# Binding the four decay differences of the SSD branch to fixed places in VectorE's queue

## The chip, the cores and the metric

The kernel runs on one core of one Trainium2 chip. The metric is the device time of one execution in microseconds, the median of several executions.

The core has five engines with a queue each: TensorE (PE in the profile; its weight loads are listed as PEld) does matrix products and transposes from SBUF into PSUM, VectorE (DVE) and ScalarE (ACT) do elementwise work, GpSimd (POOL) a few small operations, SyncE (SP) issues most DMAs.

## The reference

The network has two layers. Each is a half-step SwiGLU feed-forward part (FFN), a mixer and a second FFN; at the end stands an RMS norm. There are 256 tokens of width 1024, all in float32. The mixer runs a Mamba-2 branch (SSD) and a gated DeltaNet branch on the same input and adds their gated outputs. What matters here is the SSD branch, with 32 heads in 4 groups of 8, and two chunks of 128 tokens:

```python
a_cum = jnp.cumsum(log_a, axis=2)
seg = a_cum[:, :, :, None] - a_cum[:, :, None, :]
decay = jnp.where(causal, jnp.exp(jnp.where(causal, seg, 0.0)), 0.0)
cb = jnp.einsum("bclgn,bcsgn->bclsg", Cc, Bc)
y_diag = jnp.einsum("bclsg,bclsgh,bcsghp->bclghp", cb, decay, xdt)
...
return (y_diag + y_off).reshape(b, S, H, P)
```

For each head and chunk, `seg` is the difference of every two cumulated log decays; its exponential, masked to the causal half, is multiplied with the product of C and B, and that matrix is applied to the tokens.

## The kernel before, in words

**Weights.** All weights come from DRAM as a stream of 128 x 1024 tiles (`wraw`, 512 KB each, five buffers). Each tile is split into a rounded high part (`whi`, ScalarE, L68) and the remainder (`wlo`, VectorE, L71), so that three reduced-precision matmuls stand for one float32 matmul. High and low parts have five buffers each (`NSPL`). A tile is loaded and split ahead of its use by `take` (L202): when tile j is taken, tile j+4 is prepared. A new split thus waits until TensorE is through with the tile five before it.

**The order of the work.** A mixer is a list of small steps, `ORDER` (L46), that `step` (L1209) runs one by one. Its end, which matters here, reads `P g100 g101 D0 S0 x10 T0 D1 x11 g110 g111 S1 x20 T1 o x21 N D2 y S2 D3 x30 x31 T2 g000 g010 g001 S3 g011 T3`:

- `P` (`ssd_pre`, L1038) makes the four products of C and B (`cbb` in PSUM, L1045 and L1046). For each group VectorE masks two blocks into `cbm` (tile `cbt`, L1047), ScalarE copies a third (L1053).
- `D` and a group number (`decay`, L1059) makes that group's decay: a DMA spreads 1 MB of cumulated logs over all partitions (L1061), then come four steps over 128 x 2048 elements: the difference (VectorE, L1065), the minimum with 0 (VectorE, L1071), the exponential (ScalarE, L1072) and the product with `cbm` (VectorE, L1073). All are done in place in the tile `dc`. Groups 0 and 2 share one slot, groups 1 and 3 another.
- `S` and `T` (`ssd`, L1087) are the head and the rest of a group: transposes of the convolved input (`xsb`, L1101), three scalings (`xD`, `xdt`, `xe`), then 64 small matmuls per group that read `dc` (`ydb`, L1115), sums and a norm.
- `x` (`xs_unit`, L1076) projects half a group's input (tensor `xs`) and convolves it: for each 128 channels ScalarE starts `ca`, VectorE adds three taps (L634), ScalarE applies SiLU into `xsT` (L635). `g` (`gate`, L1141) projects a piece of a gate (PSUM name `t`).
- `o` and `N` (`dn_T`, L1150, and `dn_branch`, L1197) bring the DeltaNet result through its output matrix: four pieces are transposed (`oT`), normalised and gated (`og`) and split into `bh` (ScalarE) and `bl` (VectorE, L1160), and each pair feeds 24 matmuls into `b` (L335 to L337). The sums are gated into `tg` (L1203).
- `y` (`ss_T(0)`, L1163) transposes the first piece of the SSD result (`yT`, L1169) for its own output matrix.

The DeltaNet recurrence (`recur`, L945) ends around `P`: `ob` (L995) is added to its other part in `vb` (L998), and that addition frees a PSUM bank. The transposes and small products share four such banks (`trp`).

**What sets the order within an engine.** The code is traced once, in the order of the steps, and a scheduler then writes a fixed queue for each engine at build time. By its own estimate of times it lets the earliest traced instruction go first among those whose inputs are ready, so a later step can stand ahead of an earlier one that is not ready. `tc.issue_after(ins)` is a context: instructions of `ins`'s engine that are traced inside it stand behind `ins` in that engine's queue. It orders the queue alone and adds no semaphore. On the chip each queue is worked off in its order.

Of the kernel before, what the change touches and what calls it, by code (L numbers as in the profile page):

```python
# [11 lines left out]
ALU = mybir.AluOpType  # L12
# [4 lines left out]
P = 128  # L17
D = 1024
S = 256
# [34 lines left out]
def trunk_kernel(ctx, tc, x, wst, wsm, norms, lpar, rpar, cst, out):  # L54
    nc = tc.nc
    V, A, G, PE = nc.vector, nc.scalar, nc.gpsimd, nc.tensor
# [10 lines left out]
    def act(o, i, func=AF.Copy, **kw):  # L67
        return A.activation(out=o, in_=i, func=func, **kw)  # L68

    def tt(o, a, b, op):  # L70
        return V.tensor_tensor(out=o, in0=a, in1=b, op=op)  # L71

    def stt(o, a, s, b, op0, op1):
        return V.scalar_tensor_tensor(out=o, in0=a, scalar=s, in1=b, op0=op0, op1=op1)

    def ts(o, a, s1, op0, sc2=None, op1=None):
        if op1 is None:
            return V.tensor_scalar(out=o, in0=a, scalar1=s1, scalar2=None, op0=op0)
# [70 lines left out]
    state = {"loaded": 0, "prepped": 0, "taken": 0, "last": None, "hold": False, "behind": {}, "late": {}, "first": 0, "turns": {}, "first_chunk": False, "cap": n_forms}  # L149
# [69 lines left out]
    h = cpool.tile([P, 2, D], F32, name="h")  # L219
# [11 lines left out]
    ident = cs[:, 0:P]  # L231
# [361 lines left out]
    def mixer(l, nxt):  # L593
# [13 lines left out]
        yz = {}  # L607
# [37 lines left out]
        ac = small([P, 2, 40], "ac", 1)  # L645
# [380 lines left out]
        late = {}  # L1026
# [11 lines left out]
        def ssd_pre():  # L1038
            BT, CT = late["BC"][:, 0:4], late["BC"][:, 4:8]
            cbt = slots.tile([P, 3 * GS, P], F32, tag="sF", name="cbt")  # L1040
            late["cbx"] = cbx = cbt[:, 2 * GS :]
            late["cbm"] = cbm = cbt[:, : 2 * GS].rearrange("p (g t) l -> p g t l", g=GS)
            for g in range(GS):
                cbb = trb("cbb")
                PE.matmul(cbb[:, 0 : 2 * P], BT[:, g, 0:P], CT[:, g, :], start=True, stop=True)  # L1045
                PE.matmul(cbb[:, 2 * P : 3 * P], BT[:, g, P : 2 * P], CT[:, g, P : 2 * P], start=True, stop=True)  # L1046
                tt(  # L1047
                    cbm[:, g],
                    cbb[:].rearrange("p (t o l) -> p t o l", t=2, o=2)[:, :, 0, :],
                    U[:, None, :].to_broadcast([P, 2, P]),  # L1050
                    ALU.mult,
                )
                act(cbx[:, g], cbb[:, P : 2 * P])  # L1053
            yield

        xsT = {}
# [2 lines left out]
        def decay(g):  # L1059
            dc = slots.tile([P, 8, 2, P], F32, tag=("sA", "sB")[g % 2], name="dc")  # L1060
            nc.sync.dma_start(  # L1061
                dc[:].rearrange("p h t l -> p (h t l)"),
                rdram[8 * g : 8 * g + 8].rearrange("a b -> (a b)").partition_broadcast(P),
            )
            tt(  # L1065
                dc[:], dc[:],
                ac[:, :, 8 * g : 8 * g + 8].rearrange("p t h -> p h t")[:, :, :, None].to_broadcast([P, 8, 2, P]),
                ALU.subtract,
            )
            dv = dc[:].rearrange("p h t l -> p (h t l)")  # L1070
            ts(dv, dv, 0.0, ALU.min)  # L1071
            act(dv, dv, AF.Exp)  # L1072
            tt(dc[:], dc[:], late["cbm"][:, g, None].to_broadcast([P, 8, 2, P]), ALU.mult)  # L1073
            decs[g] = dc

        def xs_unit(g, i):  # L1076
# [73 lines left out]
        def dn_T(hp):  # L1150
            bank = trb("oT")
            bv = bank[:].rearrange("p (a c i) -> p a c i", a=2, c=4)
            for c in range(4):
                PE.transpose(bv[:, :, c, :], vb[:, c, hp, :], ident)
            og = tmp2("og")
            stt(og[:], bank[:], dnw, late["zdT"][:, 2 * hp : 2 * hp + 2, :].rearrange("p h t -> p (h t)"), ALU.mult, ALU.mult)
            oh = s2.tile([P, 2, S], F32R, tag="s2", name="bh")
            ol = s2.tile([P, 2, S], F32R, tag="s2", name="bl")
            act(oh[:].rearrange("p a t -> p (a t)"), og[:])
            tt(ol[:].rearrange("p a t -> p (a t)"), og[:], f(oh[:]).rearrange("p a t -> p (a t)"), ALU.subtract)  # L1160
            brT[("d", hp)] = (oh, ol)

        def ss_T(j):  # L1163
            bank = trb("yT")
            g, k0 = j // 2, (j % 2) * 2
            for k in range(2):
                for t in range(2):
                    c0 = (k0 + k) * P
                    PE.transpose(bank[:, k * S + t * P : k * S + (t + 1) * P], yz[g][:, t, c0 : c0 + P], ident)  # L1169
            oh = s2.tile([P, 2, S], F32R, tag="s2", name="bh")  # L1170
            ol = s2.tile([P, 2, S], F32R, tag="s2", name="bl")
            for k in range(2):
                w = snw[:, 2 * j + k : 2 * j + k + 1]
                act(oh[:, k], bank[:, k * S : (k + 1) * S], scale=w)
                stt(ol[:, k], bank[:, k * S : (k + 1) * S], w, f(oh[:, k]), ALU.mult, ALU.subtract)
            brT[("s", j)] = (oh, ol)

        def branch(kind, n, mk, tail=1):
            ps = [[accb("b"), accb("b")] for _ in range(2)]
            held = {}  # L1180

            def stat(k, t):
                oh, ol = held[k // 2]
                return oh[:, k % 2, t * P : (t + 1) * P], ol[:, k % 2, t * P : (t + 1) * P]

            made = 1
            for j0 in list(range(n - tail)) + [n - tail]:
                js = range(j0, j0 + (tail if j0 == n - tail else 1))
                while made < min(js[-1] + 2, n):
                    mk(made)  # L1190
                    made += 1
                for j in js:
                    held[j] = brT.pop((kind, j))
                out_chunks(ps, stat, [2 * j + i for j in js for i in range(2)], 2 * n - 1, group=2 * len(js))
            return ps

        def dn_branch():  # L1197
            ps = branch("d", 4, dn_T)
            m = tg[1]
            for t in range(2):  # L1200
                for n in range(2):
                    sl = slice(n * 512, (n + 1) * 512)
                    stt(m[:, t, sl], m[:, t, sl], 1.0, ps[t][n][:], ALU.add, ALU.mult)  # L1203
# [235 lines left out]
```

## Time and profile before

| | |
|---|---|
| median of 3 runs | 1543.27 us (1543.04 to 1545.02) |
| the profiled execution | 1541.48 us |
| its span, first to last instruction | 1539.7 us |
| granted TensorE clock | 0.999 |
| busy TensorE | 1522.8 us (99%) |
| busy VectorE | 1229.7 us (80%) |
| busy ScalarE | 944.8 us (61%) |

Times in the trace count from the start of the span. The end of the mixer in question lies at about 380 to 540 us in layer 0 and at 1141 to 1301 us in layer 1, with the same queues. A row in time gives the start, the duration, the engine, the line, the operation, what is written from what, and in brackets the idle time ahead of it with what ended that. A row of the chain that ended last has start, duration, engine, name and line. Small helpers record most operations, so that L71 stands for every `tt`, L68 for every `act`, L74 for every `stt` and L78 for `ts`: the names of the tiles tell them apart. For `dc`, `dc<-dc,ac` is the difference, `dc<-dc` on VectorE the minimum, `dc<-dc` on ScalarE the exponential and `dc<-dc,cbt` the product.

### The profile page before, as it was taken

The numbers are of one execution on the slowest core, as the hardware profiler recorded it, in microseconds if no ns is written. First come the engines' busy times: TensorE is split into PE (matmuls) and PEld (weight loads), VectorE is DVE, ScalarE is ACT, GpSimd is POOL, SyncE is SP. The second block draws the span as 40 slices with busy tenths as digits, with TensorE's granted clock in tenths as the row PEclk, the third lists the DMA queues.
The fourth block names the chain that finished last, engine by engine and source line by source line (L and its number), as shares of the span: only waits on it lengthen the run. The fifth ranks groups of instructions, "written<-read, shape, count | busy, mean of one in ns | idle before, by whom it ended". The sixth has DMA issues, their size and how long they took to land.

```text
span 1539.7 us, 29072 instructions
## 1 busy us (share of the span) xinstructions
PE 1522.8 (99%) x11473; PEld 1384.4 (90%) x11473; DVE 1229.7 (80%) x1859; ACT 944.8 (61%) x1532; POOL 81.8 (5%) x92
## 2 busy tenths in 40 slices
PE   8999999999999999999999999999999999999998
PEld 7999889999888888999899998899998888899997
DVE  6878769967899766789778887689589996677886
ACT  5655667765665645555555566676756666455565
POOL 0000110000000000000100012010000000000010
PEclk9999999999999999999999999999999999999999
DMA  7687775653565556587867687665345555556785
GB/s 277 190 265 231 226 228 167 187 164 111 178 213 171 163 166 196 185 256 211 261 225 225 208 253 229 197 193 180 117 141 202 179 170 186 176 177 195 247 241 156
DMA packets 98831, 305.73 MB, mean 199 GB/s; under 512 B 22837, under 2 KB 23813, under 8 KB 97670
## 3 DMA queue, kind: packets, MB, share of 16 engines
q1 hardware_dynamic: 93796, 290.95, 57.2%
q0 software_dynamic: 4608, 12.58, 5.1%
q8 instruction: 90, 1.47, 0.4%
q14 instruction: 47, 0.39, 0.1%
q10 hardware_dynamic: 290, 0.33, 0.1%
HBM read 297.72 MB, written 1.92 MB: 195 GB/s over the span
## 4 chain that ended last, share of the span: by engine, by line
PE 89%; DVE 4%; ACT 2%; DMA 2%; issue 1%; SPq 1%; POOL 0%; POOLq 0%; ACTq 0%; DVEq 0%
PE fc L346 10%; PE fc L340 9%; PE fc L345 9%; PE t L366 9%; PE o L337 4%; PE o L335 4%; PE o L336 4%; PE f L366 3%; PE b L335 3%; PE b L337 3%; PE b L336 3%; PE p L336 2%; PE p L337 2%; PE p L335 2%; PE xs L345 1%; PE xs L340 1%
## 5 line engine op out<-in xcount | busy, mean ns | idle before, releaser
L71 DVE TENSOR_TENSOR wlo<-wraw,whi 128x1024 fp32r<-128x1024 f32 x488 | 591.8, 1221 | 186.7 <-ACT whi L68 172.2
L68 ACT ACTIVATE whi<-wraw 128x1024 fp32r<-128x1024 f32 x488 | 511.6, 1059 | 271.0 <-PE fc L345 92.5
L346 PE MATMUL fc<-uW,wlo 128*128 128x256 f32 x1280 | 354.9, 277 | 0.0
L340 PE MATMUL fc<-uW,whi 128*128 128x256 f32 x1280 | 354.1, 277 | 0.0
L345 PE MATMUL fc<-uW,whi 128*128 128x256 f32 x1260 | 348.3, 276 | 0.0
L340 PEld LDWEIGHTS fc<-uW,whi 128*128 128x128 f32 x1280 | 240.5, 188 | 0.8
L346 PEld LDWEIGHTS fc<-uW,wlo 128*128 128x128 f32 x1280 | 240.5, 188 | 0.0
L345 PEld LDWEIGHTS fc<-uW,whi 128*128 128x128 f32 x1260 | 236.5, 188 | 0.8
L366 PE MATMUL t<-whi,uW 128*128 128x512 f32 x512 | 165.3, 397 | 0.0
L366 PEld LDWEIGHTS t<-whi,uW 128*128 128x128 f32 x512 | 95.9, 188 | 21.6 <-issue 1.3
L68 ACT ACTIVATE whi<-wsum 128x1024 fp32r<-128x1024 f32 x64 | 68.0, 1062 | 58.8 <-PE fc L345 32.9
L366 PE MATMUL t<-wlo,uW 128*128 128x512 f32 x256 | 100.2, 392 | 0.0
L71 DVE TENSOR_TENSOR wlo<-wsum,whi 128x1024 fp32r<-128x1024 f32 x64 | 78.2, 1221 | 7.9 <-ACT whi L68 5.6
L335 PE MATMUL b<-whi,bh 128*128 128x512 f32 x192 | 76.1, 398 | 0.3
L336 PE MATMUL b<-wlo,bh 128*128 128x512 f32 x192 | 74.9, 390 | 0.0
L337 PE MATMUL b<-whi,bl 128*128 128x512 f32 x192 | 74.2, 393 | 0.0
L340 PE MATMUL xs<-uW,whi 128*128 128x256 f32 x256 | 72.8, 284 | 0.0
L346 PE MATMUL xs<-uW,wlo 128*128 128x256 f32 x256 | 71.4, 279 | 0.0
L345 PE MATMUL xs<-uW,whi 128*128 128x256 f32 x254 | 70.6, 278 | 0.0
L335 PE MATMUL o<-whi,gh 128*128 128x512 f32 (+1 forms) x160 | 62.0, 388 | 0.0
L337 PE MATMUL o<-whi,gl 128*128 128x512 f32 (+1 forms) x160 | 61.8, 386 | 0.0
L336 PE MATMUL o<-wlo,gh 128*128 128x512 f32 (+1 forms) x160 | 61.7, 386 | 0.0
(337 smaller groups left out, 3291.7 us busy)
## 6 DMA issues: line engine op xcount, KB each, us to landing
wraw<-in_wst_dram SPq DMA_DIRECT2D x504, 512.0 KB, 4.9
wsum<-in_wst_dram SPq DMA_DIRECT2D x16, 512.0 KB, 7.3
wsum<-in_wst_dram POOLq DMA_DIRECT2D x16, 512.0 KB, 8.7
dc<-rdram SPq DMA_DIRECT2D x8, 1024.0 KB, 8.5
nw<-in_norms_dram SPq DMA_DIRECT2D x6, 512.0 KB, 5.9
h<-u POOLq DMA_DIRECT2D x12, 256.0 KB, 6.8
gb<-rdram SPq DMA_DIRECT2D x8, 256.0 KB, 5.6
h<-in_x_dram SPq DMA_DIRECT2D x4, 256.0 KB, 3.7
```

Source lines behind the costliest of these rows:

```text
L68: return A.activation(out=o, in_=i, func=func, **kw)
L71: return V.tensor_tensor(out=o, in0=a, in1=b, op=op)
L335: PE.matmul(ps, lh, rh, start=start, stop=False)
L336: PE.matmul(ps, lh, rl, start=False, stop=False)
L337: return PE.matmul(ps, ll, rh, start=False, stop=stop)
L340: PE.matmul(ps, wh, mh, start=start, stop=False)
L345: PE.matmul(ps, wh, ml, start=False, stop=False)
L346: PE.matmul(ps, wl, mh, start=False, stop=stop)
L366: ins = PE.matmul(ps[t][:], st, mv, start=k0 == 0 and j == 0, stop=k0 == KT - 2 and j == 5)
```

## The change

Two names carry instructions between the steps: `late["branch"]` and `late["diff"]`. The difference of group 0 is bound behind the fourth masked product of C and B, that of group 1 behind the minimum of group 0, that of group 2 behind the fourth `bl` of the DeltaNet branch, and that of group 3 behind the last product of group 2. The four transposes of `ss_T(0)` are bound behind the last matmul of the DeltaNet branch's sums. The computation is unchanged.

```diff
@@ ssd_pre
-                tt(
+                ins = tt(
                     cbm[:, g],
...
                 act(cbx[:, g], cbb[:, P : 2 * P])
+                if g == 3:
+                    late["branch"] = ins
@@ decay
-            tt(
-                dc[:], dc[:],
...
-                ALU.subtract,
-            )
+            with ExitStack() as behind:
+                behind.enter_context(tc.issue_after((late["diff"] if g == 1 else late["branch"]).ins))
+                tt(
+                    dc[:], dc[:],
...
+                    ALU.subtract,
+                )
             dv = dc[:].rearrange("p h t l -> p (h t l)")
-            ts(dv, dv, 0.0, ALU.min)
+            late["diff"] = ts(dv, dv, 0.0, ALU.min)
             act(dv, dv, AF.Exp)
-            tt(dc[:], dc[:], late["cbm"][:, g, None].to_broadcast([P, 8, 2, P]), ALU.mult)
+            late["branch"] = tt(dc[:], dc[:], late["cbm"][:, g, None].to_broadcast([P, 8, 2, P]), ALU.mult)
@@ dn_T
-            tt(ol[:].rearrange("p a t -> p (a t)"), og[:], f(oh[:]).rearrange("p a t -> p (a t)"), ALU.subtract)
+            ins = tt(ol[:].rearrange("p a t -> p (a t)"), og[:], f(oh[:]).rearrange("p a t -> p (a t)"), ALU.subtract)
             brT[("d", hp)] = (oh, ol)
+            if hp == 3:
+                late["branch"] = ins
@@ ss_T
-                    PE.transpose(bank[:, k * S + t * P : k * S + (t + 1) * P], yz[g][:, t, c0 : c0 + P], ident)
+                    with ExitStack() as behind:
+                        if j == 0:
+                            behind.enter_context(tc.issue_after(late["sums"].ins))
+                        PE.transpose(bank[:, k * S + t * P : k * S + (t + 1) * P], yz[g][:, t, c0 : c0 + P], ident)
@@ dn_branch
             ps = branch("d", 4, dn_T)
+            late["sums"] = state["sums"][-1]
```

More of the change, by code (lines that the diff above doesn't have):

```diff
@@ L1064, in decay @@
             )
-            tt(
-                dc[:], dc[:],
-                ac[:, :, 8 * g : 8 * g + 8].rearrange("p t h -> p h t")[:, :, :, None].to_broadcast([P, 8, 2, P]),
-                ALU.subtract,
-            )
+            with ExitStack() as behind:
+                behind.enter_context(tc.issue_after((late["diff"] if g == 1 else late["branch"]).ins))
+                tt(
+                    dc[:], dc[:],
+                    ac[:, :, 8 * g : 8 * g + 8].rearrange("p t h -> p h t")[:, :, :, None].to_broadcast([P, 8, 2, P]),
+                    ALU.subtract,
+                )
             dv = dc[:].rearrange("p h t l -> p (h t l)")
-            ts(dv, dv, 0.0, ALU.min)
+            late["diff"] = ts(dv, dv, 0.0, ALU.min)
             act(dv, dv, AF.Exp)
-            tt(dc[:], dc[:], late["cbm"][:, g, None].to_broadcast([P, 8, 2, P]), ALU.mult)
+            late["branch"] = tt(dc[:], dc[:], late["cbm"][:, g, None].to_broadcast([P, 8, 2, P]), ALU.mult)
             decs[g] = dc
```

## The prediction

> **What bounds the kernel now.** I read the page first, for the engine that sets the span; then the chain that ended last, for the places where it leaves that engine; then the rows in time around them.
>
> ```profile
> PE 1522.8 (99%) x11473; PEld 1384.4 (90%) x11473; DVE 1229.7 (80%) x1859; ACT 944.8 (61%) x1532; POOL 81.8 (5%) x92
> PE 89%; DVE 4%; ACT 2%; DMA 2%; issue 1%; SPq 1%; POOL 0%; POOLq 0%; ACTq 0%; DVEq 0%
> ```
>
> TensorE is busy for 99% and holds 89% of the chain. A reordering of VectorE can only win where TensorE stands still, and only lose by making it stand. So I looked for the places where the chain of the mixers passes through a `dc` instruction (group g's decay array; below diff, min, exp and mul are its four steps, with g behind). There are two in each layer. The first, in layer 0, begins in the chain with a DMA; behind it stand the rows in time of VectorE and TensorE, and the two TensorE rows of layer 1:
>
> ```profile
> 394.00 7.91 DMA dc<-rdram
> ...
> 401.94 2.29 DVE L71 TENSOR_TENSOR dc<-dc,ac 128x2048 f32<-128x2048 f32 x1 [0.79 <-DMA dc<-rdram]
> 404.15 0.68 DVE L71 TENSOR_TENSOR vb<-ob,os 128x512 f32<-128x512 f32 x1
> 400.93 1.16 PE L995 MATMUL ob<-vn,AT 128*128 128x128 f32 x8
> 403.80 0.48 PE L366 MATMUL t<-whi,uW 128*128 128x512 f32 x1
> 404.88 0.70 PE L1045 MATMUL cbb<-BC 128*128 128x256 f32 x2 [0.60 <-DVE vb L71]
> 1164.50 0.48 PE L366 MATMUL t<-whi,uW 128*128 128x512 f32 x1
> 1166.25 0.70 PE L1045 MATMUL cbb<-BC 128*128 128x256 f32 x2 [1.28 <-DVE vb L71]
> ```
>
> VectorE has nothing else to do when its queue reaches diff0: it waits 0.79 us for the DMA, then works 2.29 us, and the `vb` addition behind it, whose input `ob` was there at 400.93 + 1.16 = 402.09, starts only at 404.15. The fourth C·B product needs the PSUM bank that this addition frees. Starts of `t` matmuls follow each other by 0.23 us (2.30 us for ten in a row of the chain, in the next fence), so TensorE loses 404.88 - 403.80 - 0.23 = 0.85 us in layer 0 and 1166.25 - 1164.50 - 0.23 = 1.52 in layer 1.
>
> The second place is diff2, between the three taps of a convolution:
>
> ```profile
> 405.81 2.30 PE t L366 x10
> 445.15 0.12 PE xs L340
> ...
> 439.83 2.28 DVE L71 TENSOR_TENSOR dc<-dc,ac 128x2048 f32<-128x2048 f32 x1
> 442.03 0.47 DVE L74 SCALAR_TENSOR_TENSOR ca<-xs,lp,ca 128x254 f32<-128x254 f32 x1
> 443.38 0.28 PE L345 MATMUL xs<-uW,whi 128*128 128x256 f32 x1
> 444.59 0.44 PE L1101 MATMUL xsb<-cs,xsT 128*128 128x128 f32 x2 [0.93 <-ACT xsT L68]
> 1204.74 0.28 PE L345 MATMUL xs<-uW,whi 128*128 128x256 f32 x1
> 1205.95 0.44 PE L1101 MATMUL xsb<-cs,xsT 128*128 128x128 f32 x2 [0.94 <-ACT xsT L68]
> ```
>
> The last tap, ScalarE's SiLU and then the transposes of group 1 (`xsb`) wait for those 2.28 us. TensorE loses 444.59 - 443.38 - 0.12 = 1.09 us in layer 0 and 1205.95 - 1204.74 - 0.12 = 1.09 in layer 1.
>
> **The change part by part.** No instruction is added or removed; the bindings fix an order within one engine's own queue, so there is no new semaphore wait either. The dc loads are issued outside the binding: SP's queue and the landings keep their places. POOL's queue is untouched.
>
> *Group 0 behind the fourth `cbm` eviction.* The `vb` addition can start at 402.09 instead of 404.15, 2.06 us sooner; the bank is free at 402.09 + 0.68 = 402.77, before TensorE is through with the `t` matmul at 403.80 + 0.23 = 404.03. The whole stall goes: 0.85 + 1.52 us. The first product after the stall also ran slower: 0.54 us from its L1045 at 404.88 to its L1046 at 405.42, against 0.43 for the one before it, 403.23 to 403.66. That is 0.11 us in each layer, and I count it too.
>
> ```profile
> 403.23 0.60 PE L1045 MATMUL cbb<-BC 128*128 128x256 f32 x2
> 403.66 0.38 PE L1046 MATMUL cbb<-BC 128*128 128x128 f32 x2
> 405.42 0.38 PE L1046 MATMUL cbb<-BC 128*128 128x128 f32 x2
> ...
> 408.34 1.22 DVE L78 TENSOR_SCALAR dc<-dc 128x2048 f32<-128x2048 f32 x1
> 413.95 2.28 DVE L71 TENSOR_TENSOR dc<-dc,cbt 128x2048 f32<-128x2048 f32 x1
> 421.70 0.51 PE L1115 MATMUL ydb<-xdt,dc 128*64 128x64 f32 x10
> ```
>
> What this delays is diff0 itself. The fourth product now ends near 404.03 + 0.43 + 0.38 = 404.8 and its eviction near 405.3; the recurrence's last short steps come between, and I put diff0 at 405.9 to 408.2. min0 stood at 408.34, behind those same steps, so it loses nothing, and neither do exp0 on ScalarE and the steps of group 1 behind it. If this cover failed, mul0's end at 413.95 + 2.28 = 416.23 has 5.5 us to the first `ydb` matmul at 421.70, 4.5 after the gain.
>
> *Group 1 behind min0.* diff1 already stands behind min0 here, so this costs nothing.
>
> *Group 2 behind the fourth `bl`.* 2.28 us leave the convolution's chain, which was 1.09 us late, so the second stall goes whole in each layer. Nothing else that ranks low is ready there: min2 hangs on diff2, and the next split on a ScalarE step that ends later. What it may cost is where diff2, min2, mul2 now run, and that diff3 follows mul2:
>
> ```profile
> 465.81 2.28 DVE L71 TENSOR_TENSOR dc<-dc,cbt 128x2048 f32<-128x2048 f32 x1
> 470.05 2.28 DVE L71 TENSOR_TENSOR dc<-dc,ac 128x2048 f32<-128x2048 f32 x1
> 475.65 0.68 DVE L71 TENSOR_TENSOR bl<-og,bh 128x512 fp32r<-128x512 f32 x1
> 487.62 1.22 DVE L78 TENSOR_SCALAR dc<-dc 128x2048 f32<-128x2048 f32 x1
> 492.93 2.29 DVE L71 TENSOR_TENSOR dc<-dc,cbt 128x2048 f32<-128x2048 f32 x1 [0.68 <-ACT dc L68]
> 493.99 2.08 PE L1115 MATMUL ydb<-xdt,dc 128*64 128x64 f32 x64
> ```
>
> Up to 475.65 VectorE is rid of diff2, min2, mul2 and diff3, some 8 us, so the fourth `bl` can come several microseconds earlier; diff2 takes about the place of diff3 at 470, and min2 comes well before 487.62, where min3 stood: the program has D2 ahead of group 2's head S2, and D3 behind it. I estimate mul2's end at 480 to 486. Its user, `ydb` of group 2, stands at 493.99 - 2.05 = 491.9 after this layer's gain: 6 us of room. Bounds: above, the two rivals; below nothing I let it gain up to 0.6 us a layer (half the second stall) through the earlier splits, since TensorE has no third wait of that size in this stretch. I take nothing: the nearest row, mul3's, ends at 492.93 + 2.29 = 495.22, but it is of a step that ranks behind group 2's, and that had waited for group 2's to be done long before.
>
> *Group 3 behind mul2.* `ydb` of group 3 comes behind the gate chunks, one of whose matmuls stands at 508.24 (row with the first rival). Even from 490, the steps diff3, min3, exp3 with its table load, and mul3 (2.28 + 1.22 + 3.2 + 2.28 = 9.0) would end by 499, and what they push aside is the first rival. Nothing.
>
> *The transposes `yT` behind the last sum.* One of four stood among the `b` matmuls; it moves behind them with its 0.1 us. Nothing; `xsb` of group 2 queues behind them as now.
>
> [...]
>
> ```profile
> 488.59 1.07 ACT L68 ACTIVATE whi<-wraw 128x1024 fp32r<-128x1024 f32 x1 [0.29 <-PE xs L345]
> 489.68 1.28 ACT L68 ACT_TABLE_LOAD   x1
> 490.97 1.92 ACT L68 ACTIVATE dc<-dc 128x2048 f32<-128x2048 f32 x1
> ```
>
> Here the load starts 0.02 us after the `whi` before it and exp3 starts 1.29 us after the load's start, so load and exponential take 1.29 + 1.92 = 3.2 us. [...]
>
> Sum: layer 0, 0.85 + 0.11 + 1.09 = 2.05; layer 1, 1.52 + 0.11 + 1.09 = 2.72; 4.77 us in all. The profiled execution took 1541.48 us (1.78 around the span), so it would become 1536.7; the median of the runs shown, 1543.27, becomes **1538.5**.
>
> **The rivals.** *Given back by the splits (same).* The time freed before 470 can't be banked, since a split waits for one of five buffers, and then the six wide steps of groups 2 and 3 crowd the stretch behind. The first row below is that of the stretches (after the length: busy PE, PEld, DVE, ACT).
>
> ```profile
> 470.00:495.00 25.00, 25.00 (x194) 22.76 (x194) 23.97 (x26) 16.96 (x18) 0.00 (x0) 1.00 0.57 185
> ...
> 503.41 1.22 DVE L71 TENSOR_TENSOR wlo<-wraw,whi 128x1024 fp32r<-128x1024 f32 x1
> 508.24 0.39 PE L366 MATMUL t<-wlo,uW 128*128 128x512 f32 x1
> 511.73 3.50 DVE L71 TENSOR_TENSOR wlo<-wraw,whi 128x1024 fp32r<-128x1024 f32 x3 [3.30 <-ACT whi L68]
> ```
>
> VectorE is busy for 23.97 of the 25 us from 470 to 495 and without a break from there to 503.41, so it idles 1.03. The added 2.28 + 1.22 + 2.28 = 5.78 would make the split at 503.41 late by 4.75. Counting splits and chunks, its first use is the `t` matmul at 508.24, 3.61 after it ends (504.63); 1.56 after layer 0's gain and 0.89 after layer 1's. TensorE would wait up to 3.2 + 3.9 = 7.1, net +2.3: 1545.6. With half of the lag taken up by the earlier start, it waits 0.8 + 1.5 = 2.3, net -2.4: 1540.9. I put this case at the middle, 1543. Against it: 3.30 us of idle follow at once, and the bl and splits of 472 to 476 move ahead.
>
> *mul2 too late (slower).* If group 2's chain took dc3's slots, `ydb` of group 2 would wait for 495.22: 3.28 us in layer 0 (495.22 - 491.94). In layer 1, by the rows below, 1254.22 + 2.29 = 1256.51 against 1255.29 - 2.72: 3.94. It decides once mul2 ends after 491.9; the gain is gone at about 494.3.
>
> ```profile
> 451.78 1.92 ACT L68 ACTIVATE dc<-dc 128x2048 f32<-128x2048 f32 x1
> ...
> 1254.22 2.29 DVE L71 TENSOR_TENSOR dc<-dc,cbt 128x2048 f32<-128x2048 f32 x1 [0.83 <-ACT dc L68]
> 1255.29 2.08 PE L1115 MATMUL ydb<-xdt,dc 128*64 128x64 f32 x64
> ```
>
> Behind it diff3, min3 and mul3 (5.78 us) would push the split of 503.41 to end at 510.4 against a use at 508.24 + 1.23: 0.9 more in each layer. -4.77 + 7.22 + 1.9 = +4.3: 1547.6. For it: in this trace exp2 ended at 451.78 + 1.92 = 453.70 and mul2 began at 465.81, 12.1 us later, so a ready step can lie for long. Against: there it ranked below a queue that is mostly worked off by 480.
>
> *The bindings change little (same).* That could be where a binding only states the present order, as for group 1. Not for groups 0, 2 and 3, whose rows contradict the new order; only if another wide step fell into the same two gaps: 1543.
>
> **How the numbers follow.** Forecast 0.60 (1537 to 1540.1), given back 0.20, too late 0.15, little changed 0.05 (1543). A measurement tells about 0.2%, 3.1 us, from no change. Faster 0.61 (the forecast, and a sliver of the second case), same 0.23, slower 0.16. The range leaves out the slower case and a little below: 1536.5 to 1545.6.
>
> **What would show it.** Right: diff0 without a DMA wait, behind four `cbt` evictions; `cbb` and `xsb` gone from what TensorE waited for; diff2 behind the fourth `bl`; mul2 ended before `ydb` of group 2; exp2 and exp3 behind one table load, as both fall between the SiLUs of xs units 21 and 30. Wrong: a TensorE wait at `ydb` of group 2 (mul2 late), or at `t` for `wlo` near 505 (given back), or a stall at a new place from a matmul order that the new VectorE order brings with it.

## The result, and the profile after

| | before | after |
|---|---|---|
| median | 1543.45 us (6 runs, 1543.04 to 1545.02) | 1550.25 us (6 runs, 1547.94 to 1553.26) |
| ratio, 95% interval | | 1.0042 [1.0029, 1.0055] |
| the profiled execution, its span | 1541.48, 1539.7 us | 1547.94, 1546.2 us |

The change makes the kernel slower by 0.42%. The prediction was 1538.5 us, with a range up to 1545.6. All ratios are taken over undisturbed executions, which leaves out one, of the twelve of run e9 below, at 3089.99 us. The same work is done: of the page's first part and of its chain, these lines answer to those shown of before, with the same counts of instructions.

```profile
PE 1523.8 (99%) x11473; PEld 1385.7 (90%) x11473; DVE 1230.4 (80%) x1859; ACT 945.1 (61%) x1532; POOL 82.3 (5%) x92
PE 85%; DVE 7%; ACT 4%; issue 2%; DMA 1%; SPq 1%; POOL 1%; POOLq 0%; ACTq 0%; DVEq 0%
```

TensorE's share of the chain fell from 89% to 85%, VectorE's and ScalarE's rose. What TensorE waited for says where. Two lines of that view for before (each gives the total in us, how often, and the longest), then three of after:

```profile
PE cbb L1045 <- DVE vb L71: 1.9, 2, 1.3
PE xsb L1101 <- ACT xsT L68: 1.9, 2, 0.9
```

```profile
PE b L335 <- ACT bh L68: 5.2, 2, 2.7
...
PE t L366 <- DVE ca L74: 2.5, 2, 1.3
...
PE xsb L1105 <- ACT xsT L68: 1.0, 2, 0.5
```

The wait at `cbb` is gone, that at `xsb` is halved, and two new ones stand there, each in both layers: at the first `b` of the DeltaNet output (near 461 in layer 0) and at a `t` near 506.

Measured as in the prediction (from one matmul's start to the next, less the usual pace), the waits are:

| us, layer 0 / layer 1 | before | after | difference, both layers |
|---|---|---|---|
| `cbb` | 0.85 / 1.53 | none | -2.38 |
| `xsb` | 1.10 / 1.10 | 0.69 / 0.68 | -0.83 |
| first `b` | 0.31 / 0.31 | 2.87 / 2.67 | +4.92 |
| `t` near 505 | none | 1.42 / 1.44 | +2.86 |

That is +4.57 us of the 6.46 by which the spans of the two profiled executions differ. About 1.1 lies outside the two stretches: 0.48 ahead of the `ob` of layer 0 (401.41 against 400.93), the rest between the two mixers. What is left is spread over small pieces, and I did not place it.

TensorE's own place in time shows where the change won and where it lost. How much later than before it starts these matmuls (minus: earlier):

| us | layer 0 | layer 1 |
|---|---|---|
| `ob`, ahead of `cbb` | 0.48 | 4.08 |
| first `ydb` of group 0 | -0.20 | 2.74 |
| last `xs` ahead of the first `b` | -0.91 | 2.30 |
| first `ydb` of group 3 | 3.40 | 6.48 |

From the first row to the third it won 1.39 + 1.78 = 3.17 us, of the 4.77 that were forecast. From there to the last row it lost 4.31 + 4.18 = 8.49.

**The first place.** Rows of after in time, VectorE and ScalarE in layer 0, from the `vb` addition over diff0, min0, diff1, mul0 to min1, exp1, mul1:

```profile
402.61 0.69 DVE L71 TENSOR_TENSOR vb<-ob,os 128x512 f32<-128x512 f32 x1 [0.97 <-PE ob L995]
...
405.25 0.42 DVE L71 TENSOR_TENSOR cbt<-cbb,cs 128x256 f32<-128x256 f32 x1
...
407.06 2.29 DVE L71 TENSOR_TENSOR dc<-dc,ac 128x2048 f32<-128x2048 f32 x1
...
409.38 1.23 DVE L78 TENSOR_SCALAR dc<-dc 128x2048 f32<-128x2048 f32 x1
...
410.53 2.35 DVE L71 TENSOR_TENSOR wlo<-wraw,whi 128x1024 fp32r<-128x1024 f32 x2
...
412.80 2.29 DVE L71 TENSOR_TENSOR dc<-dc,ac 128x2048 f32<-128x2048 f32 x1
...
415.00 2.29 DVE L71 TENSOR_TENSOR dc<-dc,cbt 128x2048 f32<-128x2048 f32 x1
...
427.77 1.22 DVE L78 TENSOR_SCALAR dc<-dc 128x2048 f32<-128x2048 f32 x1
...
430.22 1.92 ACT L68 ACTIVATE dc<-dc 128x2048 f32<-128x2048 f32 x1
...
432.17 2.29 DVE L71 TENSOR_TENSOR dc<-dc,cbt 128x2048 f32<-128x2048 f32 x1 [0.28 <-ACT dc L68]
```

The addition goes ahead as soon as `ob` is there, and diff0 stands behind the fourth eviction without a DMA wait. But before, part of diff0's time was time in which VectorE would have waited for `ob`; now VectorE idles 0.97 us there, and the 2.29 us fall into a stretch without idle time. min0 is 1.04 us later, 0.48 of which `ob` itself is late. The same rows of before, for group 1:

```profile
409.48 2.28 DVE L71 TENSOR_TENSOR dc<-dc,ac 128x2048 f32<-128x2048 f32 x1
...
412.82 1.22 DVE L78 TENSOR_SCALAR dc<-dc 128x2048 f32<-128x2048 f32 x1
```

diff1, which two splits now overtake, is 3.3 us later, and min1, which missed its place ahead of `xdt` and the taps, 15 us: from 412.82 to 427.77. exp1 moves into the convolution, behind a table load of its own, 1.28 us at 428.92.

**The hand-over to the DeltaNet output.** Rows of VectorE, POOL and ScalarE that end in the first `b`, first of before, then of after. `sss` are the sums of SSD group 1, `srr` is POOL's power of them, `yz` ScalarE's two scalings with it; `og` to `bh` is the DeltaNet piece that `b` needs.

```profile
457.31 0.74 DVE L74 SCALAR_TENSOR_TENSOR og<-oT,lp,zdT 128x512 f32<-128x512 f32 x1
...
458.49 1.22 DVE L71 TENSOR_TENSOR wlo<-wraw,whi 128x1024 fp32r<-128x1024 f32 x1
458.66 1.61 POOL L210 TENSOR_TENSOR srr<-sss,mhalf 128x2 f32<-128x2 f32 x1 [25.77 <-DVE sss L79]
458.76 0.62 ACT L68 ACTIVATE bh<-og 128x512 fp32r<-128x512 f32 x1
...
459.44 0.50 PE L335 MATMUL b<-whi,bh 128*128 128x512 f32 x1
...
460.30 1.34 ACT L68 ACTIVATE yz<-yz,srr 128x512 f32<-128x512 f32 x2 [0.61 <-POOL srr L210]
```

```profile
455.73 0.74 DVE L74 SCALAR_TENSOR_TENSOR og<-oT,lp,zdT 128x512 f32<-128x512 f32 x1
...
456.45 2.35 DVE L71 TENSOR_TENSOR wlo<-wraw,whi 128x1024 fp32r<-128x1024 f32 x2
456.62 2.74 POOL L210 TENSOR_TENSOR srr<-sss,mhalf 128x2 f32<-128x2 f32 x1 [21.17 <-DVE sss L79]
...
459.39 1.33 ACT L68 ACTIVATE yz<-yz,srr 128x512 f32<-128x512 f32 x2 [1.96 <-POOL srr L210]
460.63 0.61 ACT L68 ACTIVATE bh<-og 128x512 fp32r<-128x512 f32 x1
...
461.30 0.50 PE L335 MATMUL b<-whi,bh 128*128 128x512 f32 x1 [2.70 <-ACT bh L68]
```

`og` is ready 1.6 us earlier than before: TensorE is 0.9 ahead, and diff2 no longer stands in VectorE's queue before it. But the sums are earlier too, and now the scheduler writes the scalings ahead of `bh` in ScalarE's queue. They wait for POOL, which takes 2.74 us beside two splits, and `bh` waits behind them: it starts at 460.63, though `og` was ready at 456.47.

**The stretch behind 470.** Rows of after: mul2, diff3, min3, mul3 on VectorE, then the last tap of the first x30 piece, ScalarE's load, SiLU and split, and TensorE's `t`:

```profile
482.28 2.29 DVE L71 TENSOR_TENSOR dc<-dc,cbt 128x2048 f32<-128x2048 f32 x1 [0.80 <-ACT dc L68]
...
490.63 2.29 DVE L71 TENSOR_TENSOR dc<-dc,ac 128x2048 f32<-128x2048 f32 x1
...
493.97 1.22 DVE L78 TENSOR_SCALAR dc<-dc 128x2048 f32<-128x2048 f32 x1
...
497.77 2.29 DVE L71 TENSOR_TENSOR dc<-dc,cbt 128x2048 f32<-128x2048 f32 x1
...
501.49 0.47 DVE L74 SCALAR_TENSOR_TENSOR ca<-xs,lp,ca 128x253 f32<-128x253 f32 x1
...
502.04 1.28 ACT L68 ACT_TABLE_LOAD   x1 [3.70 <-DVE ca L74]
503.34 0.42 ACT L68 ACTIVATE xsT<-ca 128x256 f32<-128x256 f32 x1
...
505.17 2.00 ACT L68 ACTIVATE whi<-wraw 128x1024 fp32r<-128x1024 f32 x2
...
506.50 0.47 PE L366 MATMUL t<-whi,uW 128*128 128x512 f32 x1 [1.25 <-DVE ca L74]
```

mul2 ends at 484.57, in time. Group 3's three VectorE steps stand among the taps. ScalarE waits 3.70 us for the last tap, then loads its table, and two things that `t` needs come behind all that: the split `whi`, which ends at 506.22, and one of VectorE's next taps, at 506.35, which is the one that the profile names.

### The profile page after: what moved, and what is told of

It reads as the page before. It is cut to its first block, busy times and chain, and to the rows that moved or that the text cites. A ratio compares the mean times of both kernels' runs of the same rounds, so it can differ in the third digit from the quotient of the medians.

```text
span 1546.2 us, 29072 instructions
## 1 busy us (share of the span) xinstructions
PE 1523.8 (99%) x11473; PEld 1385.7 (90%) x11473; DVE 1230.4 (80%) x1859; ACT 945.1 (61%) x1532; POOL 82.3 (5%) x92
## 4 chain that ended last, share of the span: by engine, by line
PE 85%; DVE 7%; ACT 4%; issue 2%; DMA 1%; SPq 1%; POOL 1%; POOLq 0%; ACTq 0%; DVEq 0%
PE fc L346 9%; PE fc L340 9%; PE fc L345 9%; PE t L366 9%; PE o L337 4%; PE o L335 4%; PE o L336 4%; PE f L366 3%; PE b L335 3%; PE b L337 3%; PE b L336 3%; PE p L336 2%; PE p L335 2%; PE p L337 2%; DVE wlo L71 2%
```

## The experiments

**Theory A** after this comparison: the gain of groups 0 and 1 is real, and the loss hangs on groups 2 and 3, at two separable places: ScalarE's order with POOL's power ahead of `bh`, and group 3's steps among the taps. **The rival:** in a stretch this full, any move of these wide steps reorders the queues behind it, and TensorE's waiting goes to the next place; then taking one wait away brings another. Each ratio is against executions of the kernel before taken beside the run (their medians are 1543.11 to 1544.24), so ratios compare better than medians. The larger waits of each run, as excess over the pace, layer 0 / layer 1; "bound" names the groups whose difference is bound:

| run | bound | median us | ratio [95%] | waits |
|---|---|---|---|---|
| e1_g01 | 0, 1 | 1546.26 | 1.0014 [1.0006, 1.0023] | `t` near 437 1.29 / 1.83; `xsb` 1.34 / 1.33; second `b` 0.96 / 0.97 |
| e2_g23 | 2, 3, `yT` | 1550.06 | 1.0038 [1.0025, 1.0051] | `cbb` 1.12 / 0.67; `b` 2.59 / 2.59; `t` near 505 1.56 / 1.56 |
| e3_bh_first | all | 1550.75 | 1.0041 [1.0028, 1.0053] | `xsb` 0.87 / 0.69; second `b` 1.57 / 1.79; `t` near 506 2.41 / 2.41 |
| e5_wlo_behind_bl | all | 1554.85 | 1.0066 [1.0052, 1.008] | `b` 0.84 / 0.63; near 505 1.26 + 2.41 / 1.26 + 2.41 |
| e4_d3_late | all | 1550.15 | 1.0039 [1.0027, 1.0052] | `xsb` 0.86 / 0.89; `b` 2.87 / 2.87; near 533 0.95 / 0.95 |
| e6_bh_d3 | all | 1546.93 | 1.0019 [1.001, 1.0027] | `xsb` 0.85 / 0.87; second `b` 1.59 / 1.80; `t` near 507 0.96 / 0.97 |
| e10_g01_min1 | 0, 1 | 1549.04 | 1.0031 [1.0019, 1.0043] | `xsb` 1.67 / 1.68; `b` 2.79 / 2.79 |
| e11_g2 | 2 | 1557.47 | 1.0086 [1.0073, 1.0098] | `cbb` 2.12 / 1.03; `yT` 4.36 / 5.56; `b` 1.21 / 1.21 |
| e7_vb | 0 (behind `vb`) | 1554.16 | 1.0068 [1.0056, 1.008] | `t` near 438 0.34 / 1.28; `yT` 3.05 / 3.05; `b` 1.51 / 1.51 |
| e8_xe | 2 (behind `xe`) | 1552.36 | 1.0058 [1.0046, 1.007] | `cbb` 1.72 / 0.99; `b` 4.00 / 4.00 |
| e9_vb_xe | both of these | 1544.19 | 1.0006 [0.9997, 1.0014] | `b` 1.08 / 1.29; `t` near 505 1.51 / 1.50 |
| e12_bh_d3_min1 | all | 1545.16 | 1.0016 [1.0008, 1.0025] | `xsb` 1.53 / 1.53; `b` 1.37 / 1.31; near 531 0.93 / 0.93 |
| e14_yT | `yT` | 1544.01 | 1.0002 [0.9993, 1.001] | `cbb` 0.98 / 2.25; `xsb` 1.10 / 1.10 |
| e15_g0 | 0 | 1546.95 | 1.0024 [1.0015, 1.0033] | `ydb` 1.24 / 0.27; `xsb` 1.71 / 1.72; second `b` 0.96 / 0.96 |
| e13_vb_xe_yT | as e9, `yT` | 1544.72 | 1.0012 [1.0003, 1.0021] | `b` 1.77 / 1.78; `t` near 504 1.09 / 1.08 |
| e13b_vb_xe_bh_yT | as e9, `yT` | 1545.37 | 1.0013 [1.0004, 1.0022] | as the one above |

### Halves of the change

**e1_g01** keeps groups 0 and 1 and leaves `yT` free, **e2_g23** keeps the other half; the edit in the changed kernel (e2: `g > 1`, and `yT` stays bound):

```diff
-                behind.enter_context(tc.issue_after((late["diff"] if g == 1 else late["branch"]).ins))
+                if g < 2:
+                    behind.enter_context(tc.issue_after((late["diff"] if g == 1 else late["branch"]).ins))
...
-                        if j == 0:
-                            behind.enter_context(tc.issue_after(late["sums"].ins))
```

> Groups 0 and 1 alone are bound; groups 2 and 3 and the yT transposes are free. Theory A (the loss of the change is a new wait of the first b matmul, because ScalarE has the scaling yz of group 1 ahead of bh in its queue and that scaling waits for a POOL power that stands still while VectorE splits weights; plus a wait of a t matmul near 505): in this kernel bh stands ahead of yz, so the b wait stays at 0.3 to 0.4 us, the cbb wait (0.85 and 1.52) is gone, and the time falls by 2 to 4 us, to 1539.5 to 1541.5. Rival B (only the crowding of VectorE behind 470 by groups 2 and 3 costs): the cbb wait gone and no new wait, 1538 to 1540. Rival C (moving the difference of group 0 drives the minimum and exponential of group 1 out of place, and that is the root of the loss): 1546 to 1550, with the b wait of 2 us or more.

> Groups 2 and 3 and the yT transposes are bound; groups 0 and 1 are free. Theory A: the cbb wait stays (0.85 and 1.52), the xsb wait of 1.09 goes, bh stands behind the scaling yz of group 1 in ScalarE's queue here as well, but one weight split lies beside the POOL power instead of two, so that the power takes about 1.6 us instead of 2.7 and the b wait is 1 to 1.8 us a layer; the t wait near 505 is 1 to 1.5 us; 1544 to 1547. Rival B: no b wait, the t wait alone: 1543 to 1545. Rival C: neither wait, 1541.

e1 measured 1546.26: slower, not faster. `cbb` no longer waits, but waits stand at `t` near 437 and at `xsb`, where VectorE is late with splits and taps, more than was gained. The changed kernel has no wait at `t` near 437. Rows of e1 show the difference: group 2 is free here, and its difference takes the gap between min1 and mul1, waits 0.70 us there for its load, and pushes on mul1 and the split that `t` needs:

```profile
433.11 2.29 DVE L71 TENSOR_TENSOR dc<-dc,ac 128x2048 f32<-128x2048 f32 x1 [0.70 <-DMA dc<-rdram]
435.31 2.28 DVE L71 TENSOR_TENSOR dc<-dc,cbt 128x2048 f32<-128x2048 f32 x1
...
437.58 1.22 DVE L71 TENSOR_TENSOR wlo<-wraw,whi 128x1024 fp32r<-128x1024 f32 x1
...
438.86 0.50 PE L366 MATMUL t<-wlo,uW 128*128 128x512 f32 x1 [1.12 <-DVE wlo L71]
```

So e1 does not measure what the first half is worth in the changed kernel, where diff2 stands behind 470 and TensorE still won 3.17 us up to the hand-over. As a kernel by itself, this half loses. e2 measured 1550.06 with both new waits of the changed kernel, the one at `b` larger than I expected. So the two new waits do hang on the second half.

### The two new waits, one by one and together

**e3_bh_first** issues the two scalings of group 1 behind the first `bh` on ScalarE. In `dn_T`, with the scalings of `ssd` wrapped in the function `scale`:

```diff
-            act(oh[:].rearrange("p a t -> p (a t)"), og[:])
+            ins = act(oh[:].rearrange("p a t -> p (a t)"), og[:])
+            if hp == 0:
+                with tc.issue_after(ins.ins):
+                    late["scale"]()
```

> The changed kernel with one order more: ScalarE's two scalings yz of group 1 stand behind the first bh instead of ahead of it. Theory A: the b wait falls from 2.9 to 0.3 to 0.6 us a layer, so the time falls by 4 to 5 us against the changed kernel, to 1545 to 1546, and the t wait near 505 remains. Rival B and rival C: under 1 us of change, 1549 to 1551.

The long `b` wait is gone, the time is not lower: 1550.75. 1.6 to 1.8 us now stand at the second `b` matmuls, and the `t` wait near 506 grew from 1.42 to 2.41 in each layer. The wait at the second `b` hangs on the same power: the scalings, which wait for it until 461.98, now stand ahead of the second `bh`, which starts at 464.63 though its `og` was ready at 462.06.

**e5_wlo_behind_bl** keeps ScalarE's order and takes the two splits from beside POOL's power instead, by putting them behind the first `bl`:

```diff
+            if hp == 0:
+                state["late"][state["prepped"]] = ins
+                state["late"][state["prepped"] + 1] = ins
```

> The changed kernel with ScalarE's order kept (yz ahead of bh) but the two weight splits that VectorE had right behind the sss step put behind the first bl, so that VectorE is idle beside the POOL power of group 1. Theory A: that power takes 0.7 us instead of 2.74, yz and bh come 2 us earlier, and the b wait falls from 2.9 to 0.8 to 1.2 us a layer; 1546 to 1547. A theory in which only ScalarE's order counts: the wait stays at 2.9, and the power at 2.7 us.

The first `b` wait fell from 2.87 to 0.84 (layer 1: 2.67 to 0.63): the power's length beside the splits was the larger part of it. But the two splits were wanted where they stood; 3.7 us now wait near 505 in each layer, and the time is 1554.85.

**e4_d3_late** leaves group 3's load where it is and traces its four steps behind `T2`; in the queue as built min3, exp3 and mul3 then stand behind x30's first taps (507.59 to 514.49), while diff3 (496.65) still stands ahead of the last tap. **e6_bh_d3** has this and e3's edit:

```diff
-x30 x31 T2 g000
+x30 x31 T2 e3 g000
...
             decs[g] = dc
+            if g < 3:
+                decay_steps(g)
```

> The changed kernel with the four steps of group 3 (diff, min, exp, mul) traced behind T2 instead of behind S2; its DMA stays where it is. Theory D (VectorE has no spare time from 470 to 506 in the changed kernel, since groups 2 and 3 both lie there, and the late taps of the x30 convolution make ScalarE's splits and with them a t matmul late): 5.8 us of VectorE work leave the stretch, the t wait of 1.4 us near 505 goes in both layers, the b wait of 2.7 stays, mul3 still ends before ydb of group 3; 2 to 3 us faster than the changed kernel, 1547 to 1548.5. Theory E (the waits come from the matmul order that the build-time scheduler chose, not from VectorE's load): no gain, 1549 to 1552.

> Both edits together: the scalings yz of group 1 behind the first bh, and the four steps of group 3 behind T2. Alone, the first moved the loss from the b wait to the later waits and gained nothing. Theory D: with room made behind it, its gain stays: b wait under 1 us, no t wait; cbb wait gone: 1542 to 1545.5. Theory E: as with each alone, 1548 to 1551.

In e4 the wait near 505 is gone and 0.95 us stand near 533 instead; the `b` wait is as it was, and the time is 1550.15, no lower than the changed kernel's (its clock, shown at the end, is part of that). With both edits, e6 measures 1546.93: 3.3 us better than the changed kernel, and 1.4 above what I expected. Its rows show why ScalarE's order matters: POOL's power is slower still, but nothing that TensorE's first `b` needs stands behind it.

```profile
456.59 3.34 POOL L210 TENSOR_TENSOR srr<-sss,mhalf 128x2 f32<-128x2 f32 x1 [21.25 <-DVE sss L79]
457.30 0.61 ACT L68 ACTIVATE bh<-og 128x512 fp32r<-128x512 f32 x1
...
459.96 1.34 ACT L68 ACTIVATE yz<-yz,srr 128x512 f32<-128x512 f32 x2 [2.04 <-POOL srr L210]
```

So both places were named rightly as causes of their waits, and the rival is right about the time: a wait that is taken away returns in part at the next place. In e6 too the scalings stand ahead of the second `bh` (462.60, its `og` ready at 460.03). TensorE's waits over 0.25 us in the two stretches of e6 add up to 3.5 us more than before's; its median is 3.35 above that of before taken beside it. Whether binding the scalings behind the second `bh` as well would take the 1.6 to 1.8 us away was not tried.

### Whether min1's late place is what is left

**e10_g01_min1** (e1 with group 1's difference and minimum at raised priority) and **e12_bh_d3_min1** (the same on e6):

```diff
+                if g == 1:
+                    behind.enter_context(tc.high_priority(offset=PRI))
...
-            late["diff"] = ts(dv, dv, 0.0, ALU.min)
+            with ExitStack() as behind:
+                if g == 1:
+                    behind.enter_context(tc.high_priority(offset=PRI))
+                late["diff"] = ts(dv, dv, 0.0, ALU.min)
```

> Groups 0 and 1 bound, groups 2 and 3 free, and the difference and minimum of group 1 traced at a raised priority, so that they follow the minimum of group 0 as in the kernel before, and its exponential shares a table load with that of group 0. Without the raised priority this kernel was slower than the one before by 0.14% although the cbb wait was gone: it got a t wait of 1.3 and 1.8 us near 437 and an xsb wait of 1.3. Theory D (the difference of group 0 filled VectorE's only free time there; moved, it drives minimum and exponential of group 1 into the full stretch behind): those waits shrink to under 1.1 in sum a layer, the cbb wait stays gone: 1541 to 1544. Theory E: the waits stay, 1545 to 1548.

> The changed kernel with both earlier corrections (the scalings behind the first bh, group 3's steps behind T2) and group 1's difference and minimum traced at raised priority, so that exp1 and its table load leave the convolution. If min1's late place is what keeps xsb waiting (0.85 us a layer) and makes t wait near 437, those go and the time falls from 1546.9 to 1544 or 1545. If VectorE is simply full there, the two splits that min1 overtakes come late for t instead, and the time stays at 1546 to 1549.

In both, min1 stands early again, and in e10 e1's wait at `t` near 437 is gone. But the wait at `xsb` is larger in both, 1.5 to 1.7 us, and not for one reason. In e10, where group 2 is free, diff2 stands among the taps again (441.72), as in the kernel before; a `b` wait of 2.79 comes with the new order, and the time rises from e1's 1546.26 to 1549.04. In e12 the SiLU that `xsb` needs starts 1.1 us earlier than in e6 (443.31 against 444.43), and so does `xsb` (443.78 against 444.90); the wait is longer because TensorE's queue as built has `xsb` there behind 9 `xs` matmuls and not behind 24. So min1's late place did hold `xsb` up. What its earlier place is worth is not settled: e12 measured 1545.16, the lowest with all bindings of the change and still above before, but its ratio of 1.0016 cannot be told from e6's 1.0019.

### One binding alone

**e11_g2**: `if g == 2` as in e1, `yT` free. **e15_g0**: `if g == 0`, `yT` free. **e14_yT**: no difference is bound, `yT` alone is.

> Group 2's difference alone bound, behind the fourth bl; groups 0, 1, 3 and the yT transposes free. Theory D: the cbb waits stay; the xsb wait goes; group 3's steps run where the scheduler likes, so the t wait near 505 is smaller than the 1.6 of the kernel with groups 2 and 3 bound, or gone; the b wait of 2.6 remains if ScalarE has yz ahead of bh, as it has there: 1544 to 1549. If the binding of group 3 to group 2 were what costs: 1542 to 1544.

> The kernel before with the change's first binding alone (group 0 behind the last masked product of C and B). By my prediction's sum for this part: no cbb wait, 2.6 us less, 1541. If the displaced steps are what costs, min0, min1 and the exponentials of both groups stand later still (both exponentials behind one load now), and the order at the hand-over to the DeltaNet output changes with them: waits of 1 to 4 us at xsb near 444 or at b near 460 in each layer, 1546 to 1552.

> The kernel before with one binding alone: the four transposes yT behind the last sum. VectorE's, ScalarE's and POOL's queues are those of before. If the transposes cost nothing, as I predicted, the same time within 0.1%: 1542 to 1545, with the same waits (cbb 0.85 and 1.53, xsb 1.10, b 0.31). If they filled a wait that TensorE has anyway, it becomes longer by their 0.5 us in each layer: 1544 to 1545.

e14 measured no difference (1.0002 [0.9993, 1.001]): the transposes' part of the change costs nothing. e15 and e11 are slower, by 0.24% and 0.86%, and both show something that I had not thought of. These are VectorE's queues as built, from the last splits ahead of `P` (`w` a split, `cbm` an eviction of a C and B product):

```
before   w w diff0 vb cbm cbm cbm cbm vb min0 diff1 w min1 mul0
after    w w vb cbm cbm cbm cbm vb diff0 min0 w w diff1 mul0
e15_g0   w w vb cbm diff1 cbm cbm cbm vb diff0 w w min0 min1 w mul0
```

With diff0 alone held back, diff1 takes the hole, and waits there for its own load. Rows of e15:

```profile
403.67 0.42 DVE L71 TENSOR_TENSOR cbt<-cbb,cs 128x256 f32<-128x256 f32 x1
...
405.74 2.29 DVE L71 TENSOR_TENSOR dc<-dc,ac 128x2048 f32<-128x2048 f32 x1 [1.65 <-DMA dc<-rdram]
```

mul0 then comes late (420.43), and TensorE waits 1.24 us for it at the first `ydb` (0.27 in layer 1). e15's wait at `xsb` is another matter: there the free diff2 stands among the taps (442.24), as before.

In e11, with diff2 alone held back, diff3 takes the hole ahead of the first `og`:

```profile
463.48 2.29 DVE L71 TENSOR_TENSOR dc<-dc,ac 128x2048 f32<-128x2048 f32 x1 [3.22 <-DMA dc<-rdram]
...
465.76 0.74 DVE L74 SCALAR_TENSOR_TENSOR og<-oT,lp,zdT 128x512 f32<-128x512 f32 x1
```

VectorE stands for 3.22 us with the DeltaNet piece waiting behind it, and TensorE waits over 4 us for it. With group 3 (and `yT`) bound too, in e2, that is gone and the ratio is 1.0038 instead of 1.0086. With group 1 bound too, in e1, the `ydb` wait is gone, but 1.0014 cannot be told from e15's 1.0024. So the bindings of groups 1 and 3 are not there for nothing: they close the holes that those of groups 0 and 2 open. What that is worth is shown for group 3 alone.

### Other places for the same two steps

On the kernel before, **e7_vb** binds diff0 behind the `vb` addition (`bound = {0: "vb"}`), **e8_xe** binds diff2 behind `xe` of group 1 (`{2: "xe1"}`), **e9_vb_xe** does both:

```diff
+        bound = {0: "vb", 2: "xe1"}
...
+                if g in bound:
+                    behind.enter_context(tc.issue_after(late[bound[g]].ins))
```

> The kernel before with one binding alone: group 0's difference behind the vb addition of the last chunk, ahead of the masked products of C and B. If the wait at cbb is the whole cost and the place of diff0 is free, the 0.85 and 1.52 us go and nothing comes back: 1540.5 to 1541.5. If every reordering of these wide steps moves the queues behind it (here min1 also falls behind the head of group 1, as in the changed kernel), the cbb wait goes but waits of 0.5 to 1.5 us each show up at t near 437 and at xsb near 444, as with groups 0 and 1 bound: 1543 to 1547.

> The kernel before with one binding alone: group 2's difference behind the scaling xe of group 1, which is some 10 us ahead of the place behind the fourth bl. If the far place of the changed kernel is what costs (both wide chains behind 470), the taps are freed, xsb's 1.10 us per layer go and nothing comes late: 1541 to 1542. If ScalarE's order is what costs, the scalings of group 1's result again stand ahead of the first bh in its queue, and b waits for 1 to 3 us in each layer: 1544 to 1548. The wait at cbb stays in both (0.85 and 1.52).

> Both bindings of the two single ones, no other. If each gain stands by itself, this is the sum of the two changes of time, near 1539 if both were free. If the orders disturb each other, the waits differ from the union of the single runs' and the time is 1543 to 1549.

e7 measured 1554.16, e8 1552.36, both together 1544.19. Two bindings that lose 0.68% and 0.58% alone show no loss that can be told together: the orders do not add. In e7 VectorE's queue has the sums of group 1 ahead of `og` (461.56 and 461.63); their input comes from ScalarE only at 461.24, and TensorE waits for that `og` at `yT`. In e8 the scalings again stand ahead of `bh`, and three wide VectorE steps beside POOL's power:

```profile
459.20 2.35 DVE L71 TENSOR_TENSOR wlo<-wraw,whi 128x1024 fp32r<-128x1024 f32 x2
...
459.37 3.87 POOL L210 TENSOR_TENSOR srr<-sss,mhalf 128x2 f32<-128x2 f32 x1 [23.79 <-DVE sss L79]
...
461.47 1.22 DVE L78 TENSOR_SCALAR dc<-dc 128x2048 f32<-128x2048 f32 x1
...
463.27 1.33 ACT L68 ACTIVATE yz<-yz,srr 128x512 f32<-128x512 f32 x2 [3.10 <-POOL srr L210]
464.51 0.61 ACT L68 ACTIVATE bh<-og 128x512 fp32r<-128x512 f32 x1
```

**e13_vb_xe_yT** is e9 with `yT` bound as in the change, **e13b_vb_xe_bh_yT** adds e3's edit to it; no other line differs.

> Group 0 behind vb, group 2 behind xe of group 1, and the transposes yT behind the last sum. With yT ahead of b the pair alone waited 1.1 and 1.3 us there. If the transposes themselves hold b up, this falls to 0.3 and the time from 1544.2 to 1542.5; if it is ScalarE's bh that is late, the wait stays and is longer by the transposes' 0.5 us: 1544 to 1545.

> As the one before, with ScalarE's scalings of group 1 bound behind the first bh. In this order bh already stands ahead of the scalings, so nothing moves there: the same time as the one before within 0.1%. If it differs by more than 1 us, then two kernels whose queues agree at this place differ for another reason, and the small differences in this study mean less.

1544.72 and 1545.37, with the same waits: the `b` wait is ScalarE's, and the transposes were only inside it. No version here beats the kernel before. Of those that move a difference e9 comes nearest, and cannot be told from it.

## Why the prediction was wrong, step by step

- *Group 0, the `cbb` stall:* right. 0.85 and 1.53 us went, and the first product behind runs at the usual pace (0.44 us from 404.37 to 404.81). Of the 2.6 us in the sum, 0.68 + 1.34 = 2.0 were left at the first `ydb`.
- *"min0 stood at 408.34, behind those same steps, so it loses nothing, and neither do exp0 on ScalarE and the steps of group 1 behind it":* wrong, with a small price here. I looked at whether diff0 found a place, and not at what stands behind that place: min0 came 1.04 us later (0.48 of it with `ob`), diff1 3.3, as two splits overtook it, and min1 15. In the changed kernel it cost at most the 0.6 us that are missing at the first `ydb`, and part of the gain at `xsb`. The cover that I named for mul0 held. e1, where this half alone loses 0.14% [0.06, 0.23], does not price the step, since diff2 is free there.
- *"diff1 already stands behind min0 here, so this costs nothing":* right in cost, wrong in reason. Without it diff1 takes the hole (e15).
- *Group 2, "so the second stall goes whole in each layer":* half right. 1.10 became 0.69, and e12 shows part of the reason: with min1 early, the SiLU that `xsb` needs comes 1.1 us sooner. That the freed 2.28 us go to the sums and splits, I had written down as a possible gain.
- *"since TensorE has no third wait of that size in this stretch. I take nothing":* this is the step that failed, a term put at 0 that measured +4.92 us. It had a rival for a late mul2 and none for steps that come early. The sums of group 1 came early enough to put the scalings ahead of `bh` in ScalarE's queue, where POOL's slow power held both up. e3 and e5 each removed the long wait by one link of that chain, so the chain is shown; the last sign in the prediction, a stall at a new place, pointed the right way, though it named a matmul order and had no price.
- *mul2 "at 480 to 486":* right, it ended at 484.57, and exp2 and exp3 share one table load (1.28 us at 479.04). The rival "mul2 too late", the only one that was to make the kernel slower, did not happen: the kernel is slower by another way.
- *"Group 3 behind mul2 ... Nothing":* the second step that failed, +2.86 us. It is the first rival's crowding, but the late piece is x30's taps, and with them ScalarE's `whi` and the taps that follow, not the `wlo` that I counted. e4 shows group 3's steps as its cause, not their binding: e9 and e13, where group 3 is free, wait there for 1.1 to 1.5 us too. There diff3 stands early (477.64 in e9), but min3 and mul3 (491.76, 495.17) still stand right ahead of these taps.
- *`yT`: "Nothing":* right (e14).

The trace's own account and the runs agree on the causes of the two new waits. They do not say that removing them would have won the predicted gain: e6 has neither long wait and is still slower than before by 0.19% [0.1, 0.27].

## What to carry to other kernels

A step that stands partly in idle time is cheap there, so moving it out of a critical chain is paid for at its new place: price the steps that it pushes on or that now overtake, up to the next idle time (here min0 came 1 us later, min1 15). What comes earlier is as dangerous as what comes later: look in each in-order queue for the instruction that may now overtake, and what it waits for. When one step is bound, ask which of its kind will take the hole, and expect single bindings not to add.

## What the runs showed of the hardware

**POOL's power beside VectorE.** The same instruction on 128 x 2 values took 0.70 us with no wide VectorE step beside it (after, at 434.76), 1.61 beside one split (before, at 458.66), 2.74 beside two (after, at 456.62) and 3.87 beside two splits and a minimum (e8). In the last three it ended 0.55 to 0.56 us after the last of the wide steps: before 460.27 against 459.71, after 459.36 against 458.80, e8 463.24 against 462.69. So in these rows its end follows theirs; whether it waits for them or runs slower beside them, they do not tell. Which steps lengthen it is not settled: in e6 (3.34 us) it ended 0.56 us after a `bl` behind two splits, while before it ended at 460.27 with a `bl` running from 459.63 to 460.31.

**TensorE's clock.** Behind long waits of TensorE the granted clock fell in some profiled executions and not in others. Two stretches of e4, in the first of which TensorE waits until 461.51 (length, then busy PE, PEld, DVE, ACT, POOL, then the granted clock, DMA share and GB/s), and the first of them in after, with the same wait of 2.87 us:

```profile
460.00:465.00 5.00, 3.49 (x9) 2.77 (x10) 3.51 (x6) 3.49 (x6) 0.00 (x0) 0.68 0.46 170
465.00:470.00 5.00, 5.00 (x23) 4.08 (x22) 4.27 (x9) 2.56 (x5) 0.00 (x0) 0.97 0.32 105
```

```profile
460.00:465.00 5.00, 3.70 (x16) 3.09 (x17) 3.72 (x7) 3.28 (x6) 0.00 (x0) 1.00 0.45 157
```

In e4 0.32 and 0.03 of 5.00 us of clock are missing there, 1.75 us in all, and in layer 1 1.70 us (0.66 from 1225 to 1230). In the profiled execution of after the clock is 1.00 in both places. (Its trace and that of before end lower too: 0.70 from 1540 to 1546 in after, 0.50 from 1536.0 to 1539.7 in before.) Counted in the same way, 1.70 us are missing in e8 (0.66 from 465 to 470) and 1.70 in each layer of e10 (0.85 and 0.81 from 460 to 470, 0.81 and 0.85 from 1225 to 1235). It is 3.40 in e5 (0.78 and 0.54 from 505 to 515) and 3.40 in each layer of e11 (0.65 and 0.67 from 465 to 475; 0.95, 0.50 and 0.87 from 1230 to 1245). Each is up to as much of matmul work lost, an estimate from these numbers. Over whole executions: all kernels with a single wait of 2.59 us or more at the hand-over had a mean clock between 0.994 and 0.999 (after: 1547.94 us at 0.999, 1553.26 at 0.996), and so had e5 with its 3.7 us in two pieces; the others had 0.998 to 1.000. So this is likely one reason for the spread of after's times, and part of the loss of e4, e5, e7, e8, e10 and e11. It is not what separates after from before: the spans of their two profiled executions, both with a clock of 1.00 at the ends of both mixers, differ by 6.46 us, their medians by 6.80.
